# First pass of the mixer over five row tiles, two background pieces in the fourth product, attention's first left sides in the stage of v

## The chip, the cores and the metric

The kernel runs on one core of a Trainium2 chip. The metric is the device time of one execution in microseconds (us), from start to end; where several runs are given, their median. The engines are called PE (TensorE, matrix products), PEld (its weight loads), DVE (VectorE), ACT (ScalarE), POOL (GpSimd) and SP (SyncE, which mostly issues transfers). Each engine works through its own instructions in order, and semaphores hold an instruction until what it needs is done.

## What is computed

Two layers, each with a token mixer and a dense MLP. Every part is modulated by a vector c through adaLN (shift, scale, gate). Layer 0 mixes tokens by spatial gating, layer 1 by windowed attention with three dilations. Everything is float32.

```python
def ada_mod(c, w, b):
    m = jax.nn.silu(c) @ w + b
    shift, scale, gate = jnp.split(m, 3, axis=-1)
    return shift[:, None, :], scale[:, None, :], 1.0 + gate[:, None, :]

def mixer_a(h, w_in, b_in, vn_g, vn_b, w_s, b_s, w_out):
    uv = jax.nn.gelu(h @ w_in + b_in)
    u, v = jnp.split(uv, 2, axis=-1)
    v = layer_norm(v, vn_g, vn_b)
    ...
    w_causal = jnp.where(causal, w_s, 0.0)
    z = jnp.einsum('gts,bnsgc->bntgc', w_causal, v) + b_s.T[:, :, None]
    return (u * z) @ w_out

def reference(...):
    for i in range(DEPTH):
        shift, scale, gate = ada_mod(c, ada_w[i, 0], ada_b[i, 0])
        h = x * (1.0 + scale) + shift
        y = mixer_a(...) or mixer_b(h, b_w_qkv[j], b_w_out[j], slopes)
        x = layer_norm(ALPHA * x + gate * y, ln_g[i, 0], ln_b[i, 0])
        shift, scale, gate = ada_mod(c, ada_w[i, 1], ada_b[i, 1])
        h = x * (1.0 + scale) + shift
        y = jnp.square(jax.nn.relu(h @ mlp_w_up[i])) @ mlp_w_down[i]
        x = layer_norm(ALPHA * x + gate * y, ln_g[i, 1], ln_b[i, 1])
    return x
```

x is 1024 rows by 1024 columns (eight row tiles of 128, eight column tiles k of 128), ada_w is 1024 by 3072 for each part, the MLP is 4096 wide.

## The kernel before

The program runs `mixer_a`, `mlp(1)`, `attention` and `mlp(3)` one after the other. A float32 product is made as three products of fp32r parts: `split` (L103, L104) writes a high part by a cast on ACT and a low part by a subtraction on DVE, and high x high, high x low and low x high are summed in one PSUM bank of 128x512. So one row tile with one k and one half of the columns (`dh`) costs three products. A scheduler orders the instructions of an engine, except those marked by `keep_in_program_order` (`pin`, `pe`), which keep the order of the code among themselves.

**First pass of `mixer_a` (L545 to L622).** v = gelu(h w_in + b) is made for the first 512 columns (`dh` 0) in two passes over the rows: first tiles 0 to 3, then 4 to 7 (the list `others`). In the first pass the adaLN vector of the mixer, 2048 sums over 1024 weights, isn't there yet, so the pass goes by quarters q of the model dimension (two k each). For each quarter `load` issues on SP's queue the blocks of ada_w, the row tiles' columns and one block of w_in. `add` multiplies each ada_w block by silu(c) and adds it on DVE (L587), for k = 0 to 4 (`ON_DVE`); `total` sums over the partitions on PE: twelve narrow products (one column) of raw blocks for k = 5 to 7 (L596) and four of DVE's sums with ones (L597), which DVE then adds to the bias (`mod`, L599). `turn` transposes x on PE (L535), `scaled` applies the modulation on ACT (L541), `high` casts (L545), `low` subtracts (L548), and `v_sums` makes the products (L521). All of this is pinned. The next quarter's `add` stands between the other DVE work of this one. In the second pass nothing is pinned.

After it come the spatial weights: `ws` is loaded into the work tiles with tag "h", transposed on PE (L662, `psws`), copied, and masked on POOL, ahead of the products for `dh` 1.

**Background list.** The adaLN vectors of later parts are made in pieces (`ada_steps`, L112): a group is eight steps (a load of 128x512 on SP, L123, and one DVE operation, L126 or L129), a bias row, a `reduce` (split) and a `total` on PE (`psa`, L152 to L165). `tick(n)` runs the next n pieces, `drain` all that are left. In `mlp(1)` the list has ten groups, 110 pieces. Its up stage makes seven products p for each of 16 chunks (Strassen's scheme, L915), with the left sides of five products made ahead (`AHEAD`); after each product of chunks 2 to 15 (98) it runs one piece (L992), and drains the rest (L993) before the down stage (`psd`, L1073). In these parts of j of 2 and more the steps' DVE operations are pinned.

**Attention.** `values_stage` makes v (L1267 on PE), evicted by ACT's copies (L1275) or DVE's additions (L1283) and written out by POOL's transfers (L1287). Then the PSUM banks are opened anew (set "B") and `project` makes q and k by the same seven products (`psqk`, L1426). Its `load` and first three `make_left` (`AHEAD` is 3; `left`, by L103 and L104) come after that opening. In DVE's order `far` (L1448), a copy of a mask that POOL makes (`near`, L1444), stands ahead of the low parts of these left sides.

## Time and profile before

| | us |
|---|---|
| runs of before | 2630.4, 2636.0, 2635.61 (median 2635.61) |
| profiled execution: its time | 2630.7 |
| its span, first to last instruction | 2629.0 |
| mixer's first quarter: mod(0) on DVE | 20.24 |
| the last quarter: mod(3) | 58.80 |
| second pass: first product | 73.89 |
| attention: first psqk product | 1222.08 |

The page of the profile gives busy times by engine, the groups of instructions by line and the chain of work that ended last. Beside it the trace was asked for PE's waits, for windows (busy time of each engine between two times) and for timelines (single rows: start, length, engine, line, operation, output and inputs, shape, count, and in brackets the idle time before with what ended it).

### The profile page before, as it was taken

To read this page: it belongs to the slowest core of one execution; us is meant where nothing else is said; L and a number is where in the kernel's file an instruction comes from. 1 tells how busy PE (TensorE), PEld (TensorE's weight loads), DVE (VectorE), ACT (ScalarE), POOL (GpSimd) and SP (SyncE) were. 2 spreads that over 40 slices of the span, in tenths; PEclk is the share of its full clock that TensorE was granted. 3 is DMA by queue.
4 is the path that set the end of the run, shared out by engine and by line. 5 is a ranking of instruction groups with operands and counts; after the bars stand their busy time and mean duration, and the time that the engine had idled before them with its cause. 6 is when DMAs were issued, how large, how long until landed. Compare 5 with 4: busy or idle time off the path is not lost.

```text
span 2629.0 us, 36861 instructions
## 1 busy us (share of the span) xinstructions
PE 2582.9 (98%) x13322; PEld 2079.7 (79%) x13322; DVE 1897.3 (72%) x3510; ACT 1265.9 (48%) x2436; POOL 122.0 (5%) x181
## 2 busy tenths in 40 slices
PE   7999999999999999999999999999999999999998
PEld 6778878888788888887777777777777888878887
DVE  4677798787788778444677677777669856577987
ACT  2343275555433445322655556555517655543332
POOL 0001100000000000011011011010100000000000
PEclk8999999999999999999999999999999999999999
DMA  7454427666965644542344445454853654594562
GB/s 246 119 177 127 134 102 249 205 220 220 309 233 176 228 141 151 160 160 96 98 115 134 121 119 158 135 142 135 316 175 110 222 186 148 173 328 155 184 207 81
DMA packets 328779, 453.37 MB, mean 172 GB/s; under 512 B 51420, under 2 KB 179844, under 8 KB 328596
## 3 DMA queue, kind: packets, MB, share of 16 engines
q1 hardware_dynamic: 316692, 409.07, 48.8%
q0 software_dynamic: 11904, 41.95, 4.5%
q8 instruction: 104, 1.70, 0.3%
q14 instruction: 79, 0.65, 0.1%
HBM read 342.33 MB, written 108.61 MB: 172 GB/s over the span
## 4 chain that ended last, share of the span: by engine, by line
PE 82%; DVE 7%; issue 6%; DMA 3%; ACT 1%; POOL 1%; SPq 0%; DVEq 0%; POOLq 0%; ACTq 0%
PE psd L1073 20%; PE psqk L1426 18%; PE psua L915 11%; PE psuc L915 6%; PE psv L1267 4%; PE psv L521 3%; PE psd_wout L329 3%; PE psd_wo L329 3%; PE psub L915 3%; PE psu L329 3%; PE sc L1579 2%; PE pv L1619 2%; DMA adaw<-in_ada_w_dram 2%; PE pT L1590 1%; DVE right L104 1%
## 5 line engine op out<-in xcount | busy, mean ns | idle before, releaser
L1426 PE MATMUL psqk<-right,left 128*128 128x512 f32 x2016 | 523.1, 404 | 3.3 <-DVE left L104 2.2
L1426 PEld LDWEIGHTS psqk<-right,left 128*128 128x128 f32 x2016 | 363.1, 189 | 96.0 <-issue 14.9
L915 PE MATMUL psua<-right,left 128*128 128x512 f32 x1536 | 364.6, 391 | 3.2 <-ACT right L103 1.8
L1073 PE MATMUL psd<-rhi,lhi 128*128 128x512 f32 x896 | 350.8, 392 | 2.3 <-ACT part L946 2.1
L1073 PE MATMUL psd<-rlo,lhi 128*128 128x512 f32 x896 | 350.3, 391 | 0.7 <-DVE rlo L104 0.6
L1073 PE MATMUL psd<-rhi,llo 128*128 128x512 f32 x896 | 350.1, 391 | 0.0
L915 PEld LDWEIGHTS psua<-right,left 128*128 128x128 f32 x1536 | 287.1, 188 | 65.2 <-DVE right L104 2.6
L104 DVE TENSOR_TENSOR left<-ws,left 128x512 fp32r<-128x512 f32 x224 | 153.6, 687 | 141.4 <-ACT left L103 139.8
L1267 PE MATMUL psv<-vwhi,right 128*128 128x512 f32 x672 | 209.8, 393 | 0.0
L1493 ACT ACTIVATE p<-p,stat 128x256 f32<-128x256 f32 (+2 forms) x384 | 161.8, 423 | 90.7 <-DVE stat L1491 89.0
L1073 PEld LDWEIGHTS psd<-rhi,lhi 128*128 128x128 f32 x896 | 168.9, 189 | 38.7 <-ACT part L946 3.0
L1073 PEld LDWEIGHTS psd<-rlo,lhi 128*128 128x128 f32 x896 | 169.0, 189 | 36.6 <-DVE rlo L104 1.5
L1073 PEld LDWEIGHTS psd<-rhi,llo 128*128 128x128 f32 x896 | 168.9, 189 | 34.8
L915 PE MATMUL psuc<-right,left 128*128 128x512 f32 x768 | 189.5, 393 | 0.5 <-ACT right L103 0.4
L103 ACT CAST left<-ws 128x512 fp32r<-128x512 f32 x224 | 137.9, 620 | 102.5 <-DVE ws L836 73.7
L915 PEld LDWEIGHTS psuc<-right,left 128*128 128x128 f32 x768 | 144.5, 189 | 31.4 <-DVE right L104 0.9
L129 DVE SCALAR_TENSOR_TENSOR adaacc<-adaw,silu_c,adaacc 128x512 f32<-128x512 f32 x140 | 107.3, 766 | 63.3 <-DMA adaw<-in_ada_w_dram 62.3
L1267 PEld LDWEIGHTS psv<-vwhi,right 128*128 128x128 f32 x672 | 126.0, 188 | 28.0 <-ACT vwhi L103 0.2
L1491 DVE CUSTOM_DVE_ANT_0 p<-sc,bias 128x256 f32<-128x256 f32 (+2 forms) x384 | 103.5, 325 | 55.4 <-PE sc L1579 55.3
L104 DVE TENSOR_TENSOR llo<-lraw,lhi 128x1024 fp32r<-128x1024 f32 x112 | 136.2, 1216 | 1.5 <-ACT lhi L103 1.5
L1267 PE MATMUL psv<-vwlo,right 128*128 128x512 f32 x336 | 131.9, 394 | 0.2 <-DVE vwlo L104 0.2
L103 ACT CAST lhi<-lraw 128x1024 fp32r<-128x1024 f32 x112 | 117.3, 1048 | 7.6 <-PE psua L915 4.3
(266 smaller groups left out, 4354.1 us busy)
## 6 DMA issues: line engine op xcount, KB each, us to landing
lraw<-forms SPq DMA_DIRECT2D x112, 512.0 KB, 4.0
adaw<-in_ada_w_dram SPq DMA_DIRECT2D x192, 256.0 KB, 3.2
up<-in_mlp_w_up_dram SPq DMA_DIRECT2D x64, 512.0 KB, 3.9
forms<-s SPq DMA_DIRECT2D x128, 256.0 KB, 2.3
rraw<-in_mlp_w_down_dram SPq DMA_DIRECT2D x64, 512.0 KB, 5.9
forms<-part SPq DMA_DIRECT2D x96, 256.0 KB, 2.5
vraw<-in_b_w_qkv_dram SPq DMA_DIRECT2D x42, 512.0 KB, 4.0
spill<-acc SPq DMA_DIRECT2D x24, 512.0 KB, 2.6
```

Of the source, the lines that this page charges most:

```text
L103: first = A.copy(hi, src) if hi_engine is A else hi_engine.tensor_copy(hi, src)
L104: return first, lo_engine.tensor_tensor(lo, src, hi, op=ALU.subtract)
L129: ins = V.scalar_tensor_tensor(acc[:], raw[:], silu_c[:, k : k + 1], acc[:], ALU.mult, ALU.add)
L329: T.matmul(dst, s[a], m[b], start=(n == 0), stop=(n == last))
L521: pin(T.matmul(sums[half, dh, i][:], hT[half][a][:, k, i * P : (i + 1) * P], w[b][:, k % 2, :], start=k == 0 and a + b == 0, stop=k == KD ...
L915: T.matmul(acc, w[:, a, k, :], right[p][:, b, k, :], start=p in (1, 2, 5) and k + a + b == 0, stop=k == 3 and a == 1, skip_group_check=True)
L1073: T.matmul(sums[kind, m][:], l[a][:, k, m * P : (m + 1) * P], r[b][:, k, :], start=p in (1, 5, 2, 3) and kp + k + a + b == 0, stop=kp == K ...
L1267: T.matmul(sums[own, m][:], right[p][:, b, 2 * kp + k, m * P : (m + 1) * P], w[a][:, k, :], start=new and k + a + b == 0, stop=kp + k == 2 ...
L1426: ins = T.matmul(sums[kind][:], w[:, a, k, :], right[p][:, b, k, :], start=p in (1, 2, 5) and k + a + b == 0, stop=k == 3 and a == 1, skip ...
L1491: V.tensor_tensor_reduce(out=pr, in0=src, in1=bias, scale=-0.125, scalar=3e38, op0=ALU.add, op1=ALU.min, accum_out=nm)
L1493: A.activation(pr, pr, AF.Exp, bias=nm, scale=-1.0, accum_out=l)
L1579: pe(T.matmul(scb[e][:, sl], my["q"][rows, t * P : (t + 1) * P], my["k"][rows, k0 : k0 + w], start=True, stop=True))
```

## The change

1. The mixer's first pass takes five row tiles (`FIRST`), the second three. The row tiles' columns are loaded on POOL's queue (`nc.gpsimd`), ahead of the ada_w blocks in the code; a block of ada_w is now one k with both parts (128x2x256, 256 KB), and the loads of w_in are pinned too. `add` covers all eight k, with one operation 512 wide for both parts. `total` is left with four narrow products, written into the third transposing bank (`extra`), which also holds the fifth tile's transposes; the transposes now stand ahead of the sums. The last tile of `others` no longer takes a tile of the pool `ada0`.
2. The spatial weights' loads and transposes are spread over the k of `dh` 1 (half 1).
3. In the up stage of `mlp` the fourth product of a chunk runs two pieces of the background list.
4. `project` is defined ahead of `values_stage`; its first loads (into work tiles with tag "res") and the first two left sides are issued within the last steps of that stage, the third after the banks are opened.

Parts of the diff (the definitions that only move are left out):

```diff
+            def v_sums(dh, k, rows_, pin=free):
                 w = w_units[dh, k // 2]
-                for i in range(4):
...
-                ON_DVE = 5
+                FIRST = range(5)
...
-
-                    for kk in range(3):
-                        for part in (1, 0):
-                            block(kk, part)
-                    w = slice(q * QUARTER, (q + 1) * QUARTER)
-                    for i in range(4):
-                        pin(nc.sync.dma_start(tiles[i][:, w], x_in[i * P : (i + 1) * P, w]))
-                    w_raw[q] = v_raw(0, q)
-                    for part in (1, 0):
-                        block(3, part)
+                    cols_ = slice(q * QUARTER, (q + 1) * QUARTER)
+                    parts = ada_w[0, 0].rearrange("k (s n) -> k s n", n=D)[:, 0:2, cols_]
+
+                    def block(k):
+                        t = raws[q, k] = ada0.tile([P, 2, QUARTER], F32, name=f"adaw_0_{q}_{k}", tag="adaw", bufs=16)
+                        pin(nc.sync.dma_start(t[:], parts[k * P : (k + 1) * P]))
+
+                    for i in FIRST:
+                        pin(nc.gpsimd.dma_start(tiles[i][:, cols_], x_in[i * P : (i + 1) * P, cols_]))
+                    for k in range(KD - 2):
+                        block(k)
+                    w_raw[q] = v_raw(0, q, pin)
+                    for k in range(KD - 2, KD):
+                        block(k)
 
...
                 def add(q, ks):
                     for k in ks:
-                        for part in (1, 0):
...
-
-                def total(q):
-                    pst = bank("tr", f"psa_0_{q}")
-                    for part in range(2):
+                        if k == 0:
+                            accs[q] = ada0.tile([P, 2, QUARTER], F32, name=f"adaacc_0_{q}", tag="adaacc")
+                            pin(V.tensor_scalar(accs[q][:], raws[q, 0][:], silu_c[:, 0:1], None, ALU.mult))
+                        else:
+                            acc = accs[q][:]
+                            pin(V.scalar_tensor_tensor(acc, raws[q, k][:], silu_c[:, k : k + 1], acc, ALU.mult, ALU.add))
+
+                def total(q, pst):
+                    for s in range(2):
                         for n in range(2):
-                            c = slice(2 * part + n, 2 * part + n + 1)
+                            c = slice(2 * P + 2 * s + n, 2 * P + 2 * s + n + 1)
                             w = slice(n * P, (n + 1) * P)
-                            for k in range(ON_DVE, KD):
-                                pin(T.matmul(pst[:, c], raws[q, part, k // 2][:, k % 2, w], silu_c[:, k : k + 1], start=k == ON_DVE, stop=False))
-                            pin(T.matmul(pst[:, c], accs[q, part][:, w], ones_f[:, 0:1], start=False, stop=True))
+                            pin(T.matmul(pst[:, c], accs[q][:, s, w], ones_f[:, 0:1], start=True, stop=True))
...
-                add(0, range(ON_DVE))
                 load(1)
+                add(0, range(KD - 2))
+                every = slice(0, HALF)
                 for q in range(4):
-                    total(q)
-                    psts = [turn(0, k, tiles, pin) for k in (2 * q, 2 * q + 1)]
-                    h = scaled(0, 2 * q, psts[0], pin)
-                    high(0, 2 * q, h, pin)
+                    k0, k1 = 2 * q, 2 * q + 1
+                    psts = [bank("tr", f"pst_0_{k}") for k in (k0, k1)]
+                    for k in (k0, k1):
+                        turn(psts[k % 2], 0, k, tiles[:4], pin)
+                    extra = bank("tr", f"pst_0_x{q}")
+                    for k in (k0, k1):
+                        turn(extra, (k % 2) * P, k, tiles[4:], pin)
+                    add(q, range(KD - 2, KD))
+                    v_split(0, q, w_raw[q], pin)
+                    total(q, extra)
+                    h = [h_tile(f"h_0_{k}") for k in (k0, k1)]
+                    scaled(h[0][:], psts[0][:], k0, pin)
+                    high(0, k0, every, h[0][:], pin)
                     if q:
-                        v_sums(0, 0, 2 * q - 1, pin)
+                        v_sums(0, k0 - 1, FIRST, pin)
                     if q < 3:
-                        add(q + 1, range(2))
-                    low(0, 2 * q, h, pin)
-                    v_split(0, q, w_raw[q], pin)
-                    h = scaled(0, 2 * q + 1, psts[1], pin)
-                    high(0, 2 * q + 1, h, pin)
+                        add(q + 1, range(1))
+                    low(0, k0, every, h[0][:], pin)
+                    scaled(h[1][:], psts[1][:], k1, pin)
+                    high(0, k1, every, h[1][:], pin)
                     if q < 3:
-                        add(q + 1, range(2, 3))
-                    low(0, 2 * q + 1, h, pin)
-                    v_sums(0, 0, 2 * q, pin)
+                        add(q + 1, range(1, 2))
+                    low(0, k1, every, h[1][:], pin)
+                    hx = h_tile(f"h_0_x{q}")
+                    for k in (k0, k1):
+                        w = slice((k % 2) * P, (k % 2 + 1) * P)
+                        scaled(hx[:, w], extra[:, w], k, pin)
+                    both = hx[:, 0 : 2 * P].rearrange("p (k c) -> p k c", c=P)
+                    high(1, slice(k0, k1 + 1), slice(0, P), both, pin)
+                    low(1, slice(k0, k1 + 1), slice(0, P), both, pin)
+                    v_sums(0, k0, FIRST, pin)
                     if q < 2:
                         load(q + 2)
                     if q < 3:
-                        add(q + 1, range(3, ON_DVE))
-                v_sums(0, 0, KD - 1, pin)
+                        add(q + 1, range(2, KD - 2))
+                v_sums(0, KD - 1, FIRST, pin)
...
-                others = [work.tile([P, D], F32, name=f"x0_{4 + i}", tag="res", bufs=3) for i in range(3)]
-                others.append(ada0.tile([P, D], F32, name="x0_7", tag="x0"))
+                others = [work.tile([P, D], F32, name=f"x0_{5 + i}", tag="res", bufs=3) for i in range(3)]
                 for i, t in enumerate(others):
-                    nc.sync.dma_start(t[:], x_in[(4 + i) * P : (5 + i) * P, :])
-                v_end(0, 0)
+                    nc.sync.dma_start(t[:], x_in[(5 + i) * P : (6 + i) * P, :])
+                v_end(0, FIRST)
+                rest = slice(P, HALF)
                 for k in range(KD):
-                    h = scaled(1, k, turn(1, k, others))
-                    high(1, k, h)
-                    low(1, k, h)
-                    v_sums(1, 0, k)
-                v_end(1, 0)
+                    pst = bank("tr", f"pst_1_{k}")
+                    turn(pst, P, k, others)
+                    h = h_tile(f"h_1_{k}")
+                    scaled(h[:, rest], pst[:, rest], k)
+                    high(1, k, rest, h[:, rest])
+                    low(1, k, rest, h[:, rest])
+                    v_sums(0, k, range(5, NT))
+                v_end(0, range(5, NT))
...
+                raw_s = {}
+
+                def spatial_load(q):
+                    ws = raw_s[q] = work.tile([P, 4, P], F32, name=f"ws_{q}", tag="h")
                     nc.sync.dma_start(ws[:], a_w_s[0, 4 * q : 4 * q + 4].rearrange("g t s -> t g s"))
+
+                def spatial(q):
+                    ws = raw_s.pop(q)
...
+                        if half and 3 <= k < 7:
+                            spatial(k - 3)
+                        if half and 1 <= k < 5:
+                            spatial_load(k - 1)
+                        v_sums(1, k, range(4 * half, 4 * half + 4))
...
-                        tick()
+                        tick(2 if p == 4 else 1)
...
+            def two(name):
+                t = work.tile([P, 2, 4, P], F32, name=name, tag="res", bufs=3)
+                return [t[:, 0], t[:, 1]]
...
+                lefts = [(n, p) for n in range(len(order)) for p in (1, 2, 6, 5, 7, 4, 3)]
+                yield
+                for s in lefts[: AHEAD - 1]:
+                    make_left(*s)
+                yield
+                make_left(*lefts[AHEAD - 1])
...
+                        if n in (len(steps) - LOADS, len(steps) - SPLITS):
+                            next(stream)
...
-                for s in lefts[:AHEAD]:
-                    make_left(*s)
```

**Place 1: PE, the first pass, about the sums of quarter 1.** The first rows are the second half of the sum. Names: psv are the sums of v (row tile in the name), psa the modulation's sums, adaacc DVE's sums, pst the banks of the transposes. Before:

```order
L597 MATMUL psa_1_283<-ones_f,adaacc_1_0_226 128x1
L596 MATMUL psa_1_283<-silu_c,adaw_1_1_2_178 128x1
L596 MATMUL psa_1_283<-silu_c,adaw_1_1_3_188 128x1 x2
L597 MATMUL psa_1_283<-ones_f,adaacc_1_1_224 128x1
L596 MATMUL psa_1_283<-silu_c,adaw_1_1_2_178 128x1
L596 MATMUL psa_1_283<-silu_c,adaw_1_1_3_188 128x1 x2
L597 MATMUL psa_1_283<-ones_f,adaacc_1_1_224 128x1
L535 MATMUL pst_0_2_302<-ident,x_0_132 128x128
```

Now, where pst_x is the fifth row tile's bank:

```order
L522 MATMUL psv_4_247<-winv_0_hi,hT_1_1_124 128x512
L535 MATMUL pst_2_278<-ident,x_0_132 128x128
L535 MATMUL pst_2_278<-ident,x_1_133 128x128
L535 MATMUL pst_2_278<-ident,x_2_134 128x128
L535 MATMUL pst_2_278<-ident,x_3_135 128x128
L535 MATMUL pst_3_279<-ident,x_0_132 128x128
L535 MATMUL pst_3_279<-ident,x_1_133 128x128
L535 MATMUL pst_3_279<-ident,x_2_134 128x128
L535 MATMUL pst_3_279<-ident,x_3_135 128x128
L535 MATMUL pst_x_288<-ident,x_4_136 128x128 x2
L591 MATMUL pst_x_288<-ones_f,adaacc_1_219 128x1 x4
L522 MATMUL psv_0_231<-winv_0_hi,hT_0_0_121 128x512
```

The twelve products with adaw are gone, the four with adaacc are left, and the transposes, ten instead of eight, stand ahead of them.

**Place 2: PE, between the up and the down stage of the first MLP.** psa_0_1 is the last sum of the background list (hi and lo parts of adaacc), psu the up stage's products, psd the down stage's. Before, inside the down stage:

```order
L1073 MATMUL psd_1_0_5971<-rhi_1_3_6041,llo_1_3_6038 128x512
L1073 MATMUL psd_1_1_5975<-rhi_1_3_6041,lhi_1_3_6037 128x512
L1073 MATMUL psd_1_1_5975<-rlo_1_3_6042,lhi_1_3_6037 128x512
L160 MATMUL psa_0_1_5890<-ones_r,adahi_0_1_5886 128x2
L1073 MATMUL psd_1_1_5975<-rhi_1_3_6041,llo_1_3_6038 128x512
L1073 MATMUL psd_1_2_5979<-rhi_1_3_6041,lhi_1_3_6037 128x512
L1073 MATMUL psd_1_2_5979<-rlo_1_3_6042,lhi_1_3_6037 128x512
L1073 MATMUL psd_1_2_5979<-rhi_1_3_6041,llo_1_3_6038 128x512
```

Now, inside the up stage:

```order
L937 MATMUL psua_15_5688<-right_7_3168,left_15_7_5685 128x512 x12
L937 MATMUL psuc_15_5733<-right_3_2971,left_15_3_5707 128x512 x12
L160 MATMUL psa_0_1_5834<-ones_r,adahi_0_1_5806 128x2
L937 MATMUL psua_15_5688<-right_4_3169,left_15_4_5730 128x512
L161 MATMUL psa_0_1_5834<-ones_r,adalo_0_1_5807 128x2
```

The sum moved from between products of the down stage to between the last two products of the up stage.

**Place 3: DVE, the end of v's stage in attention.** vwlo is the low part of the last weights of v, v_0 the evictions of v, left the low parts of q's and k's left sides, ws sums of weights, far the copy that waits for POOL. Before:

```order
L104 TENSOR_TENSOR vwlo_4_1_9930<-vraw_4_1_0_9891,vwhi_4_1_9929 128x1024
L1283 TENSOR_TENSOR v_0_0_9782<-psv_0_0_9653,v_0_0_9782 128x512
L1283 TENSOR_TENSOR v_0_1_9784<-psv_0_1_9657,v_0_1_9784 128x512
L1283 TENSOR_TENSOR v_0_2_9786<-psv_0_2_9661,v_0_2_9786 128x512
L1283 TENSOR_TENSOR v_0_3_9788<-psv_0_3_9665,v_0_3_9788 128x512
L1448 COPY far<-near 64x64 x2
L104 TENSOR_TENSOR left_2_1_10024<-wq_0_2_10016,left_2_1_10024 128x512
L104 TENSOR_TENSOR left_2_2_10027<-wq_0_2_10018,left_2_2_10027 128x512
L1370 TENSOR_TENSOR ws_2_6_10030<-wk_0_2_10020,wk_0_2_10022 128x512
L1198 TENSOR_TENSOR ws_2_6_10031<-ws_2_6_10030,wq_0_2_10016 128x512
```

Now:

```order
L1440 TENSOR_TENSOR v_0_0_9745<-psv_0_0_9616,v_0_0_9745 128x512
L1440 TENSOR_TENSOR v_0_1_9747<-psv_0_1_9620,v_0_1_9747 128x512
L1440 TENSOR_TENSOR v_0_2_9749<-psv_0_2_9624,v_0_2_9749 128x512
L1440 TENSOR_TENSOR v_0_3_9751<-psv_0_3_9628,v_0_3_9751 128x512
L104 TENSOR_TENSOR left_2_2_9929<-wq_2_9896,left_2_2_9929 128x512
L1292 TENSOR_TENSOR ws_2_6_9991<-wk_2_9899 128x512
L1220 TENSOR_TENSOR ws_2_6_9991<-ws_2_6_9991,wq_2_9896 128x512
L104 TENSOR_TENSOR left_2_6_9994<-ws_2_6_9991,left_2_6_9994 128x512
L104 TENSOR_TENSOR left_2_5_10001<-ws_2_6_9991,left_2_5_10001 128x512
L1220 TENSOR_TENSOR ws_2_7_10033<-wk_2_9899,ws_2_6_9991 128x512
L1220 TENSOR_TENSOR ws_2_6_9991<-wq_2_9896,ws_2_6_9991 128x512
L1485 COPY far<-near 64x64 x2
```

The low parts of the left sides 1, 2, 6 and 5 now stand ahead of far; left_2_1's stands in the row ahead of the first one shown, ahead of the last evictions of v.

More of the change, by code (lines that the diff above doesn't have):

```diff
@@ L522, in v_sums, with v_end @@
                                      start=k == 0 and a + b == 0, stop=k == KD - 1 and a == 1))
[L524 removed]
+            def v_end(dh, rows_):
                 w = slice(dh * HALF, (dh + 1) * HALF)
[L526 to L528 removed]
+                for r in rows_:
+                    z = vz[:, r, w]
+                    V.tensor_tensor(z, sums.pop((dh, r))[:], v_bias[:, w], op=ALU.add)
@@ L538, in scaled @@
-            def scaled(half, k, pst, pin=free):
-                h = work.tile([P, HALF], F32, name=f"h_0_{half}_{k}", tag="h")
+                    pin(T.transpose(pst[:, c0 + n * P : c0 + (n + 1) * P], t[:, k * P : (k + 1) * P], ident[:]))
+            def scaled(dst, src, k, pin=free):
                 m = mods[k // 2]
-                pin(A.activation(h[:], pst[:], AF.Identity, bias=m[:, k % 2 : k % 2 + 1], scale=m[:, 2 + k % 2 : 3 + k % 2]))
-                return h
-            def high(half, k, h, pin=free):
-                pin(A.copy(hT[half][0][:, k, :], h[:]))
@@ L547, in low, with high @@
-            def low(half, k, h, pin=free):
-                pin(V.tensor_tensor(hT[half][1][:, k, :], h[:], hT[half][0][:, k, :], op=ALU.subtract))
-            with tc.tile_pool(name="ada0", bufs=2, reuse_waits="tile") as ada0:
-                ON_DVE = 5
+                pin(A.activation(dst, src, AF.Identity, bias=m[:, k % 2 : k % 2 + 1], scale=m[:, 2 + k % 2 : 3 + k % 2]))
+            def high(half, ks, cols_, h, pin=free):
+                pin(A.copy(hT[half][0][:, ks, cols_], h))
+            def low(half, ks, cols_, h, pin=free):
+                pin(V.tensor_tensor(hT[half][1][:, ks, cols_], h, hT[half][0][:, ks, cols_], op=ALU.subtract))
@@ L553, in pin, with h_tile @@
+            def h_tile(name):
+                return work.tile([P, HALF], F32, name=name, tag="h")
+            with tc.tile_pool(name="ada0", bufs=3, reuse_waits="tile") as ada0:
+                FIRST = range(5)
                 def pin(ins):
@@ L1206, in values_stage @@
+            stream = project()
             def values_stage():
@@ L1328, in by_pos @@
-            def by_pos(t, g):
-                if g == 0:
-                    return t
-                if g == 1:
-                    return t.rearrange("p (i r) -> p r i", r=4)
-                return t.rearrange("p (i b a) -> p a b i", b=2, a=8)
-            order = [(hp, g) for hp in range(N_PAIRS) for g in PATTERNS]
-            got = [dict() for _ in order]
-            pinned = []
-            def quarter(name):
-                return qp.tile([P, 4, P], F32, name=name, tag="wq", bufs=4)
```

241 lines of the change are left out of this document (117 added, 124 removed).

## The prediction

> **What bounds the kernel.** I read the busy times first, then what TensorE (PE) waited for, then windows over the stretches that the change touches.
>
> ```profile
> PE 2582.9 (98%) x13322; PEld 2079.7 (79%) x13322; DVE 1897.3 (72%) x3510; ACT 1265.9 (48%) x2436; POOL 122.0 (5%) x181
> ```
>
> PE is busy for 98% of the span, so a faster vector or scalar engine brings nothing by itself. Time can come only from three places: PE work that is dropped, PE idle time, and PE work done at a low granted clock. Which waits exist, the view of PE's waits says (what waited, for what: us in all, times, the longest):
>
> ```profile
> PE psa L596 <- DMA adaw<-in_ada_w_dram: 8.2, 2, 4.8
> PE psqk L1426 <- DVE left L104: 2.2, 1, 2.2
> PE psqk L1426 <- ACT left L103: 1.2, 1, 1.2
> PE psws L662 <- DMA ws<-in_a_w_s_dram: 0.9, 1, 0.9
> ```
>
> What a dense product costs, and what it costs at the low clock, two rows of the chain of work that ended last show (start, length, engine, what, count):
>
> ```profile
> 24.88 5.06 PE psv L521 x11
> ...
> 74.04 13.79 PE psv L521 x60
> ```
>
> At full clock a 128x512 product takes 13.79/60 = 0.230 us; in the first stretch it took 5.06/11 = 0.46, exactly twice.
>
> **Mixer, first pass: the sums for the modulation.** Windows on PE's psa work alone, one for each quarter (sum, PE, PEld, DVE, mean granted clock, DMA share, GB/s):
>
> ```profile
> 13.60:20.10 6.50, 6.46 (x30) 6.46 (x30) 0.00 (x0) 1.00 1.01 321
> 29.70:33.40 3.70, 3.67 (x32) 3.66 (x31) 0.00 (x0) 1.00 1.01 330
> 41.30:46.00 4.70, 4.62 (x32) 4.66 (x32) 0.00 (x0) 0.75 0.99 342
> 54.40:58.70 4.30, 4.21 (x32) 4.23 (x32) 0.00 (x0) 0.83 0.01 4
> ```
>
> The four stretches hold PE for 6.5 + 3.7 + 4.7 + 4.3 = 19.2 us (the first mostly waits for adaw). The change leaves 8 of 32 records: 3.67 x 8/32 = 0.9 us each at the rate of the second, some 1.7 at half clock. In exchange DVE adds all eight k instead of five. So the period of a quarter passes from PE to DVE, and I add up DVE's and ScalarE's (ACT's) chain. Groups by form (count | busy, mean ns | idle before):
>
> ```profile
> L129 DVE SCALAR_TENSOR_TENSOR adaacc<-adaw,silu_c,adaacc 128x512 f32<-128x512 f32 x70 | 52.3, 747 | 23.7 <-DMA adaw<-in_ada_w_dram 23.4
> L126 DVE TENSOR_SCALAR adaacc<-adaw,silu_c 128x512 f32<-128x512 f32 x10 | 4.8, 478 | 0.0
> L548 DVE TENSOR_TENSOR hT<-h,hT 128x512 fp32r<-128x512 f32 x10 | 6.8, 687 | 5.2 <-ACT hT L545 5.2
> L104 DVE TENSOR_TENSOR winv_lo<-winv_raw,winv_hi 128x1024 fp32r<-128x1024 f32 x4 | 4.9, 1225 | 1.0 <-ACT winv_hi L103 0.8 <-DMA x<-in_x_dram 0.3
> L541 ACT ACTIVATE h<-pst,mod 128x512 f32<-128x512 f32 x16 | 12.1, 774 | 46.2 <-PE pst L535 45.3 <-DVE hT L548 0.9
> L545 ACT CAST hT<-h 128x512 fp32r<-128x512 f32 x16 | 9.6, 619 | 0.3
> ```
>
> From one modulation (mod) to the next: scale 0.77 and cast 0.62 on ACT, low part 0.69 on DVE; the add of k=1, 0.75; the second low part until 3.7; the fifth row's narrow scale, cast and low part (no such form before; between nothing and three full operations of 2.1, I take 0.8, by width) until 4.5; six adds of 0.75 until 9.0; the split of w_in 1.23, beside which PE's short sum lies; then mod. That is 10.3, and I take 10.5. PE has 30 products x 0.23 = 6.9, ten transposes of 0.12 (1.47/12, row below) and the sum of 0.9 in that time, 9.0 at full clock: it fits, closely. The row tile that is new in this pass so costs PE nothing here.
>
> Next, when the first quarter can begin. The start's windows (PE, PEld, DVE, ACT, POOL, then clock, DMA share, GB/s) and mod's rows:
>
> ```profile
> 0.00:10.00 10.00, 0.71 (x3) 0.48 (x3) 4.81 (x18) 1.49 (x2) 0.70 (x6) 1.00 0.67 203
> 10.00:20.00 10.00, 6.65 (x32) 6.56 (x32) 0.27 (x1) 0.00 (x0) 0.00 (x0) 1.00 1.03 338
> 20.00:30.00 10.00, 7.93 (x24) 6.00 (x24) 6.37 (x14) 3.64 (x5) 0.00 (x0) 1.00 1.02 328
> ...
> 20.24 0.16 DVE L599 TENSOR_TENSOR mod<-psa,bias 128x4 f32<-128x4 f32 x1 [9.97 <-PE psa L597]
> ...
> 58.80 0.16 DVE L599 TENSOR_TENSOR mod<-psa,bias 128x4 f32<-128x4 f32 x1 [5.06 <-PE psa L597]
> ```
>
> From 10 to 30 us the 16 DMA engines are full, at 338 GB/s. All 2.62 MB of x (five rows, four quarters) now stands at the head of GpSimd's (POOL's) queue, beside 2.62 MB of quarter 0 on SP's. If both share the engines evenly, 5.24 MB must have moved: 2.03 MB by 10 us, the other 3.21 MB at 0.338 MB/us by 19.5 us. One add, the sum and mod: 21.3, a little later than the 20.24 of before. Bounds are 16 (x takes nothing from SP) and 25 (x goes ahead of it). The Trainium skill ("DMA: Bandwidth & Descriptors", Issuing engines are not separate DMA queues) says that DMAs of every issuing engine run on the same 16 engines and interleave, and that a second issuer saves only issue time. By that rule the move itself buys nothing and mod stands at 21.3; without it at 16, five us better. That the share was full with SP alone speaks for the rule; how POOL's packets mix in, no row of before shows.
>
> How long POOL takes to issue, a later place shows:
>
> ```profile
> 1054.20 2.58 POOL L1287 DMA_DIRECT2D v_dram<-v  x4 [8.28 <-DVE v L1283]
> ```
>
> That is 0.65 us each, 13 us for the 20; they wait for nothing, and nothing else that POOL does is needed in this stage. Then mod(3) = 21.3 + 11.5 (a cold first quarter, as the row of x11 shows) + 10.5 + 10.5 = 53.8 against 58.80. Behind it stand 45 products, 10.4, and about 0.9 of low clock: the pass ends at 65. Before:
>
> ```profile
> 70.44 1.47 PE L535 MATMUL pst<-ident,x 128*128 128x128 f32 x12
> ...
> 73.89 0.50 PE L521 MATMUL psv<-winv_hi,hT 128*128 128x512 f32 x1
> ```
>
> The second pass's products then begin at 65 + 3.1 = 68.1 (3.45 before, less one row's share of the first transposes), not at 73.89: 5.8 gained. It has three rows, not four: 24 products less, 5.5, and 0.4 of transposes. Together 11.7; I take **11.5** (7 to 15). The move of the spatial loads takes away the wait of psws: **0.9**.
>
> **MLP: two pieces in the fourth product.** The background list of 110 pieces has 98 places in the up stage; 12 are drained after it, and the last sum of the list then stands among the down products. With two pieces in 14 places there are 112. The windows at that place, and the wait:
>
> ```profile
> 684.00:688.00 4.00, 2.81 (x13) 2.00 (x11) 1.80 (x3) 2.12 (x2) 0.00 (x0) 1.00 0.98 309
> 688.00:692.00 4.00, 2.11 (x13) 1.93 (x14) 3.01 (x6) 1.08 (x2) 0.00 (x0) 1.00 1.01 388
> 692.00:696.00 4.00, 4.00 (x12) 3.09 (x12) 4.00 (x6) 2.68 (x3) 0.00 (x0) 0.57 1.05 393
> ...
> 689.89 0.27 PE L160 MATMUL psa<-ones_r,adahi 128*128 128x2 f32 x1 [3.08 <-ACT adahi L103]
> ```
>
> In these 12 us PE did 38 records, 8 of them the narrow sum: 30 products, 6.9 us at full rate. 5.1 are lost, first by waiting, then at a clock of 0.57. The sum itself, 0.9, only moves: **4.2** (2 to 5). It could wait in the up stage as well, for an adaw that lands late; that would be some 1 us.
>
> **Attention: the first left sides.** At the opening PE waits twice:
>
> ```profile
> 1218.82 2.69 ACT L1275 COPY v<-psv 128x512 f32<-128x512 f32 x4 [19.19 <-PE psv L1267]
> 1222.08 0.73 PE L1426 MATMUL psqk<-right,left 128*128 128x512 f32 x2 [1.19 <-ACT left L103]
> ...
> 1223.80 0.39 DVE L1448 COPY far<-near 64x64 f32<-64x64 f32 x2 [13.42 <-POOL near L1444]
> ...
> 1224.96 11.39 PE L1426 MATMUL psqk<-right,left 128*128 128x512 f32 x42 [2.15 <-DVE left L104]
> ```
>
> The casts stand behind ACT's copies of v, the low parts behind DVE's copy far, which waits for POOL. With both made ahead of that, 44 products run from 1220.89 (1222.08 less 1.19) and end after 44 x 0.23 = 10.1 at 1231.0; they ended at 1224.96 + 11.39 = 1236.35. That is **5.2** (3 to 5.4): 3.3 of waiting, the rest low clock. The DVE work ahead of far is cover for the third left side; if it lay late, the 2.15 would come back.
>
> **Sum.** 11.5 + 0.9 + 4.2 + 5.2 = 21.8. The profiled execution took 2630.7 (its span 2629.0): 2608.9. The runs of before lie at 2630.4, 2635.61 and 2636.0, so their median is 4.9 above the profiled one, and the sum would be 2613.8 from there. I forecast **2611**, between the two, nearer the profile.
>
> **Rivals.**
> Low clock in each quarter: ten transposes and a sum stand between the products in every quarter, and after such stretches (41 to 46 us) the clock was 0.75. If each of the three later quarters loses what the 11 products at half rate lost (5.06/2 = 2.5), it is 7.6 less the 0.9 that I allowed, 6.7: 2618. The Trainium skill ("TensorE: Matmul & The Clock Gate", Part 1: The HAM clock gate) says that the clock is reconsidered in windows of about 3.4 us, and halves after an idle one. The trace agrees, with 0.46 beside 0.230 us for a product; by that rule a quarter in which PE idles little, 1.5 of 10.5 us, would mostly keep its clock, which is why this is not the forecast. Chance 0.2.
> x ahead of adaw: mod(0) at 25, or SP's blocks starved in a later quarter, 4 to 7 us: 2616 to 2618. For it: the share is full for 30 us. Against: POOL's issues come one in 0.65 us, so that x is spread over 13 us. Chance 0.12.
> Parts that don't do what they say: the third left side still late (2.2 and its low clock), or the last sum waits among the up products: 2 to 4 us, 2614. Chance 0.1.
> POOL's queue takes nothing from SP's: mod(0) at 16, 2606. Chance 0.1.
> Slower: the additions of the background list are pinned on DVE in program order, so one that waits for its adaw holds what is queued behind it, the low parts of the next left sides, and PE waits for these.
>
> ```profile
> adaw<-in_ada_w_dram SPq DMA_DIRECT2D x192, 256.0 KB, 3.2
> ```
>
> With two pieces in 14 places, each could wait the 3.2 us of a landing: 44.8. Less the other 17.6 that is 27 slower: 2658. It decides once the waits exceed the cover of five products made ahead, 5 x 12 x 0.23 = 13.8 us. One landing is far below that. Chance 0.03.
>
> **How the numbers follow.** The forecast's own case (2606 to 2614) has 0.45. Range 2602 to 2621: it takes in the good rival and the two at 2616 to 2618. About 0.2% (5.3 us) is what a measurement of this kernel can tell from no change; slower 0.03, within it 0.03 (two of the larger rivals together with weak gains elsewhere), faster 0.94.
>
> **What would show it.** mod(0) near 21 and mod(3) near 54 in the rows of DVE; psa's windows of 1 to 2 us each; the second pass's products from 68; DMA share full until 20 in the first windows; no idle time at the opening of attention and 44 products in 10 us; no psa among the down products. Wrong it would be if mod's period is over 12, if the clock is below 0.8 in every quarter, or if DVE waits long for adaw in the MLP's up stage.

## The result and the profile after

| | before | after |
|---|---|---|
| median of the runs, us | 2635.05 (4 runs) | 2613.59 (4 runs, 2611.85 to 2616.89) |
| ratio, 95% interval | | 0.9924 (0.9906 to 0.9941) |
| profiled execution: time, span | 2630.7, 2629.0 | 2611.85, 2610.1 |

The change makes the kernel 0.8% faster in this comparison, and 0.6% in a second one (after_again below). The page of the profile after, the line of busy times by engine:

```profile
PE 2561.9 (98%) x13226; PEld 2058.5 (79%) x13226; DVE 1902.3 (73%) x3506; ACT 1267.7 (49%) x2448; POOL 132.8 (5%) x201
```

PE lost 96 records (the 12 narrow products of four quarters, recorded twice each) and 21 us of busy time; DVE's busy time is 5 us longer, and POOL has its 20 issues more. PE's waits after, those that answer to the ones of before:

```profile
PE pst_x L591 <- DVE adaacc L584: 10.3, 2, 9.0
...
PE psa L161 <- DVE adalo L104: 1.8, 2, 1.5
...
PE psa L160 <- ACT adahi L103: 1.2, 2, 0.8
```

The waits for adaw, for the left sides and for ws are gone. The first row is the start of the first quarter (9.0) and a wait of 1.2 in the third. The two rows of psa are four waits in the up stage of the first MLP (0.23 + 0.43 + 1.54 + 0.78 = 3.0 us), where the kernel before has none; of them more below.

**The first pass.** The modulation's rows on DVE (start, length, engine, line, operation, what, count, idle time before), and two windows of the start:

```profile
21.74 0.16 DVE L593 TENSOR_TENSOR mod<-pst_x,bias 128x4 f32<-128x4 f32 x1 [0.82 <-PE pst_x L591]
...
32.04 0.16 DVE L593 TENSOR_TENSOR mod<-pst_x,bias 128x4 f32<-128x4 f32 x1
...
42.35 0.16 DVE L593 TENSOR_TENSOR mod<-pst_x,bias 128x4 f32<-128x4 f32 x1
...
52.76 0.16 DVE L593 TENSOR_TENSOR mod<-pst_x,bias 128x4 f32<-128x4 f32 x1
```

```profile
0.00:10.00 10.00, 2.56 (x9) 1.60 (x10) 2.72 (x11) 1.49 (x2) 6.92 (x18) 1.00 0.73 218
10.00:20.00 10.00, 0.96 (x5) 0.56 (x3) 4.48 (x7) 1.04 (x1) 4.72 (x9) 1.00 1.07 359
```

mod(0) stands at 21.74, the period is 10.3, mod(3) at 52.76: forecast were 21.3, 10.5 and 53.8. The three middle intervals have the same length to 0.1 us and the rows 2 to 4 show no idle time before them: DVE works without a break toward mod, as the sum of its chain said. In the first 20 us PE does almost nothing (3.5 of 20 us), and from 10 to 20 us the DMA share is 1.07.

**Between the stages of the first MLP, and inside the up stage.** Windows (sum, PE, PEld, DVE, ACT, POOL, clock, DMA share, GB/s), first the stretch behind the up stage, then two inside it:

```profile
682.00:686.00 4.00, 4.00 (x20) 3.30 (x19) 0.82 (x1) 2.00 (x2) 0.00 (x0) 1.00 1.04 393
```

```profile
598.00:602.00 4.00, 2.02 (x12) 1.56 (x12) 3.98 (x9) 1.70 (x4) 0.00 (x0) 1.00 0.71 240
602.00:606.00 4.00, 4.00 (x13) 3.10 (x12) 2.54 (x5) 2.15 (x4) 0.00 (x0) 0.61 0.98 313
```

The loss between the stages is gone, as forecast. A new one stands inside the up stage: PE idles for half of one window and runs at a clock of 0.61 in the next. The rows around it, on PE and on DVE:

```profile
598.53 0.27 PE L160 MATMUL psa<-ones_r,adahi 128*128 128x2 f32 x1 [0.43 <-ACT adahi L103]
600.68 0.27 PE L161 MATMUL psa<-ones_r,adalo 128*128 128x2 f32 x1 [1.54 <-DVE adalo L104]
```

```profile
597.07 0.75 DVE L129 SCALAR_TENSOR_TENSOR adaacc<-adaw,silu_c,adaacc 128x512 f32<-128x512 f32 x1 [1.91 <-DMA adaw<-in_ada_w_dram]
...
599.94 0.69 DVE L104 TENSOR_TENSOR adalo<-adaacc,adahi 128x512 fp32r<-128x512 f32 x1
```

The last addition of a background sum waited 1.91 us for its adaw; its low part came 2.9 us later, behind other work of DVE; and the sum's products, which the order has between products of the up stage, held PE.

**Attention.** PE's row and one of ACT's:

```profile
1207.15 13.07 PE L1351 MATMUL psqk<-right,left 128*128 128x512 f32 x56
```

```profile
1195.88 0.62 ACT L103 CAST left<-wq 128x512 fp32r<-128x512 f32 x1 [4.82 <-PE psv L1424]
```

56 products of psqk run without a break, 0.233 us each, and the left side was cast 11 us ahead of them.

### The profile page after: what moved, and what is told of

It is laid out like the page before. It is cut to its first block, busy times and chain, and to the rows that moved or that the text cites. A ratio compares the mean times of both kernels' runs of the same rounds, so it can differ in the third digit from the quotient of the medians.

```text
span 2610.1 us, 36711 instructions
## 1 busy us (share of the span) xinstructions
PE 2561.9 (98%) x13226; PEld 2058.5 (79%) x13226; DVE 1902.3 (73%) x3506; ACT 1267.7 (49%) x2448; POOL 132.8 (5%) x201
## 4 chain that ended last, share of the span: by engine, by line
PE 85%; DVE 7%; DMA 4%; ACT 2%; issue 1%; SPq 0%; DVEq 0%; ACTq 0%
PE psd L1095 23%; PE psqk L1351 17%; PE psua L937 10%; PE psv L1424 9%; PE psuc L937 5%; PE psu L329 3%; DMA adaw<-in_ada_w_dram 3%; PE psd_wout L329 3%; PE psd_wo L329 3%; PE psub L937 2%; PE sc L1616 2%; PE pv L1656 2%; PE psv L522 1%; PE pT L1627 1%; DVE right L104 1%; DVE left L104 1%
```

## The experiments

The total times scatter by some 5 us from run to run, so beside the ratios I use the starts of the same PE instructions in the profiles. In this table u is the first product of psu (end of the mixer's v stage), MLP the time from the first psua product to the 101st psd product (the background list's last sum lies in it), attention that from the 1001st product of psv in the program (the 617th of attention) to the 45th of psqk. The three times of a row are those of one profile.

| run | what it is | u, us | MLP, us | attention, us | ratio to before (95%) |
|---|---|---|---|---|---|
| before | | 147.9 | 349.7 | 105.8 | 1 |
| after | the change | 135.4 | 350.5 | 100.4 | 0.9924 (0.9906 to 0.9941) |
| after_again | the change | 133.5 | 352.7 | 100.4 | 0.9941 (0.9928 to 0.9954) |
| e1_one_piece | part 3 undone | 135.1 | 354.4 | 100.4 | 0.9940 (0.9924 to 0.9955) |
| e2_spaced | split a piece earlier | 135.3 | 349.6 | 100.4 | 0.9938 (0.9924 to 0.9951) |
| e3_x_on_sp | x on SP | 134.8 | 351.7 | 100.4 | 0.9951 (0.9937 to 0.9965) |
| e4_four_rows | four row tiles | 136.5 | 353.0 | 100.4 | 0.9969 (0.9958 to 0.9981) |
| e6_all_dve | before, sums on DVE | 138.6 | 351.2 | 106.0 | 0.9985 (0.9974 to 0.9996) |
| e11_late_sums | sums two pieces later | 133.8 | 347.8 | 100.4 | 0.9917 (0.9904 to 0.9930) |
| e9_three_bufs | three adaw buffers | 131.1 | 345.3 | 100.4 | 0.9898 (0.9885 to 0.9910) |
| e10_three_bufs_one | the same, part 3 undone | 132.0 | 351.0 | 100.4 | 0.9922 (0.9906 to 0.9939) |
| e13_three_bufs_x | e9, later x on SP | 128.6 | 347.2 | 100.4 | 0.9897 (0.9880 to 0.9914) |
| e15_bufs_x_sp | e9, all x on SP | 129.7 | 346.9 | 100.4 | 0.9899 (0.9882 to 0.9916) |
| e14_four_rows_bufs | e9, four row tiles | 133.0 | 345.2 | 100.4 | 0.9914 (0.9897 to 0.9931) |

The start of the first quarter scatters too, which u contains: in the seven profiles whose first pass is the same code (after, after_again, e1, e2, e11, e9, e10) mod(0) stands at 19.6 to 21.7 us. Where it matters I also count u from the run's own mod(0).

**Part 3 undone.**

```diff
-                        tick(2 if p == 4 else 1)
+                        tick()
```

> The change with one background piece after every product again (part 3 undone). By the prediction's term, part 3 is worth 4.2 us, so this is 4.2 slower than the changed kernel, about 2618. By the ledger of the two traces, part 3 gave its gain between the stages back inside the up stage (a wait of 1.5 us on adalo at 600.7 us and a half-clock window from 602.9 us, then a wait of 0.8 at 656.6): the two cancel, this runs within 1 us of the changed kernel, 2613, with a half-clock window shortly after the up stage and none near 600 us.

The medians agree within the scatter, 2612.89 here and 2613.97 for the change run once more (the kernel before had 2630.07 and 2630.05 beside them). In the trace the up stage is clean, and the loss stands behind it again. PE's row with the wait, and the windows around it:

```profile
677.62 0.37 PE L160 MATMUL psa<-ones_r,adahi 128*128 128x2 f32 x1 [3.08 <-ACT adahi L103]
```

```profile
676.00:680.00 4.00, 2.38 (x8) 1.99 (x8) 2.71 (x4) 1.66 (x2) 0.00 (x0) 0.58 1.02 380
680.00:684.00 4.00, 4.00 (x13) 3.42 (x14) 2.76 (x5) 2.09 (x2) 0.00 (x0) 0.50 1.06 395
684.00:688.00 4.00, 4.00 (x13) 3.11 (x13) 2.01 (x2) 0.76 (x1) 0.00 (x0) 0.64 1.05 392
```

The wait is the 3.08 us of before, to the digit, but the low clock behind it lasts longer: the three windows add up to 10.2 us at half rate, and before it was 3.4 (4 us at 0.57). That is why the MLP takes 354.4 us here (one short stretch of low clock near 363 us, 1.6, is in it too), against 349.7 in the kernel before with the same order. Against this run, part 3 brought 1.7 to 3.9 us (1.7 to 2.3 without the stretches of 1.6 near 363 us here and near 360 us in after_again); against the one profile of before, nothing.

**The split a piece earlier.**

```diff
-            todo.append([lambda k=k, step=step: step(k) for k in range(KD)] + [bias_row, reduce, total])
+            todo.append(steps_[:-1] + [lambda s=steps_[-1], r=bias_row: (s(), r()), reduce, lambda: None, total])
```

(The second line holds for the parts of j of 2 and more; the others keep the first.)

> The change, with one empty piece between the split of a background sum (reduce) and its psa products on PE; the bias row's piece is joined to the eighth addition, so there are still 110 pieces. If psa comes too close behind its split, PE gains a product of 2.7 us as cover: the waits at 600.7 and 656.6 and the half-clock window go, 5 to 6 us less, about 2608. If instead DVE is simply too far behind in that stage, the waits turn up at other products and the time stays within 2 us of 2613.

Neither: the waits did not go, nor did they move.

```profile
598.60 0.27 PE L160 MATMUL psa<-ones_r,adahi 128*128 128x2 f32 x1 [0.29 <-ACT adahi L103]
600.75 0.27 PE L161 MATMUL psa<-ones_r,adalo 128*128 128x2 f32 x1 [1.54 <-DVE adalo L104]
```

An earlier split can't start before the last addition, and that one waits for its adaw. So it is not the distance of split and sum in the list that decides; the distance of the last addition and the sum, three pieces, is the same in both. The theory of the expectation fell. (No low-clock window followed here, which alone is worth some 1.5 us.)

**x on SP's queue.**

```diff
-                    for i in FIRST:
-                        pin(nc.gpsimd.dma_start(tiles[i][:, cols_], x_in[i * P : (i + 1) * P, cols_]))
                     for k in range(KD - 2):
                         block(k)
+                    for i in FIRST:
+                        pin(nc.sync.dma_start(tiles[i][:, cols_], x_in[i * P : (i + 1) * P, cols_]))
```

> The change with the five x loads of a quarter on SP's queue again, behind the six first adaw blocks of that quarter. If queue and issuing engine matter little because the 16 engines are full (share 1.07 from 10 to 20 us), mod(0) stays at 20 to 22 us and the time within 2 us of 2613. If POOL's queue takes the x bytes of later quarters in front of adaw, mod(0) comes some 3 to 5 us earlier here and the time is 2609 to 2611. If SP's issue time (20 issues of 0.5 us or more) is what counts, mod comes later by 3 or more in each quarter and the time is over 2618.

The four rows of mod together (count: least, median and longest ns; first and last start):

```profile
L593 DVE TENSOR_TENSOR mod<-pst_x,bias x4: 160/163/164, 21.7 to 52.7; 128x4 f32<-128x4 f32 x4
```

The modulation comes at the same times. But the run tells less than it was meant to: with SP's pinned loads changed, the scheduler had put two whole row tiles of the second pass (1 MB) ahead of x on SP. e15 below repeats it with that order held.

**Four row tiles in the first pass.**

```diff
-                FIRST = range(5)
+                FIRST = range(4)
...
-                    v_sums(0, k, range(5, NT))
+                    v_sums(0, k, range(4, NT))
```

(The fifth tile's transposes and narrow operations are left out, and a fourth tile is loaded for the second pass.)

> The change with four row tiles in the first pass and four in the second; the rest as changed. If DVE's chain sets a quarter (10.3 us, of which the fifth row's narrow operations are 0.9), mod(3) comes some 2.6 us earlier and the second pass takes 5.9 us longer: 3.3 slower than the changed kernel, about 2617. If PE's products set it, each quarter is 1.4 us shorter and nearly all of the 5.9 is won back: 2613 to 2615. If five rows bring their full 5.9: 2619.

The rows of mod together, and a row of PE in the u stage:

```profile
L593 DVE TENSOR_TENSOR mod<-pst_x,bias x4: 161/162/163, 21.4 to 49.8; 128x4 f32<-128x4 f32 x4
```

```profile
161.24 0.27 PE L160 MATMUL psa<-ones_r,adahi 128*128 128x2 f32 x1 [1.93 <-ACT adahi L103]
```

mod(3) comes 2.9 us earlier, near the 2.6 of the first case: DVE's chain sets a quarter. At u the loss is 1.0 us against the first profile of the change (2.9 against the second); counted from each run's own mod(0) it is 1.4 and 1.6. The rest of the 7 us by which the medians differ comes later: a late background split in the u stage (the second row) and low clock behind it, and a longer MLP.

**The change again, and the sums two pieces later.**

```diff
-            later(ada_steps(2, MODS + GATE) + ada_steps(3, MODS))
+            groups = ada_steps(2, MODS + GATE) + ada_steps(3, MODS)
+            for g in range(len(groups) - 1):
+                groups[g + 1].insert(2, groups[g].pop())
+            groups[-1].insert(len(groups[-1]) - 1, lambda: None)
+            later(groups)
```

> The changed kernel once more, beside the next three on one chip, so that they can be compared with it directly: 0.992 of the kernel before.

> The change with each background sum's psa products run two pieces later than now (after the second addition of the next group), the last one a piece later. e2 left psa in its place on PE, since it only moved the split. If psa waits because the last addition, held by a late adaw, leaves its split too little time, two more products (5.5 us) cover it: the waits at 600.7 and 656.6 us go, the half-clock window near 603 too, the MLP keeps 4 to 6 us more than the changed kernel, in all 0.2% less. If PE waits for DVE in that stage anyway, nothing changes.

The change again: 2613.97, and 2608.38 with the later sums (before 2630.05). The MLP takes 347.8 us instead of 350.5 and 352.7. The sum that waited now reads:

```profile
601.01 0.17 PE L160 MATMUL psa<-ones_r,adahi 128*128 128x2 f32 x1
```

No idle time stands before it, nor before any other sum of that stage. So the new waits can be covered by moving the sum, which is what e2 failed to do. A wait of 1.15 us for an eviction by DVE (at 650 us) and a stretch of low clock at 657 us are left.

**Three buffers for adaw.**

```diff
-                raw = ada_p.tile([P, HALF], F32, name=f"adaw_{nm}_{k}", tag="adaw", bufs=2)
+                raw = ada_p.tile([P, HALF], F32, name=f"adaw_{nm}_{k}", tag="adaw", bufs=3)
```

(The bias row, which takes a tile with the same tag, has 3 too.)

> The change with three buffers for the background list's adaw blocks, not two, so that a load can be issued one piece earlier. If the late adaw is the cause of the waits of psa, DVE's wait of 1.9 us ahead of the addition at 597 us goes and with it the 2.0 us of psa's wait and the half-clock window: 4 to 5 us less in the MLP. If the place of psa alone decides, the waits stay.

The cause itself: groups by form of DVE in the up stage (340 to 665 us), first of before (count | busy, mean ns | idle before):

```profile
L129 DVE SCALAR_TENSOR_TENSOR adaacc<-adaw,silu_c,adaacc 128x512 f32<-128x512 f32 x63 | 47.0, 746 | 19.0 <-DMA adaw<-in_ada_w_dram 18.7
```

of after:

```profile
L129 DVE SCALAR_TENSOR_TENSOR adaacc<-adaw,silu_c,adaacc 128x512 f32<-128x512 f32 x70 | 52.3, 747 | 25.4 <-DMA adaw<-in_ada_w_dram 25.2
```

and of this run:

```profile
L129 DVE SCALAR_TENSOR_TENSOR adaacc<-adaw,silu_c,adaacc 128x512 f32<-128x512 f32 x70 | 52.1, 744 | 8.8 <-DMA adaw<-in_ada_w_dram 8.8
```

DVE's waits for adaw rose from 18.7 to 25.2 us with the denser list and fall to 8.8 with a third buffer. By themselves they hold PE little: they are 28.4 us in e11, where no sum waits. They cost where a sum stands close behind the addition that waits. With the third buffer PE has no wait in the two windows that were shown of the change:

```profile
598.00:602.00 4.00, 4.00 (x20) 3.30 (x19) 0.31 (x1) 1.87 (x4) 0.00 (x0) 1.00 0.47 157
602.00:606.00 4.00, 4.00 (x19) 3.32 (x18) 3.18 (x6) 1.81 (x4) 0.00 (x0) 1.00 0.40 133
```

The MLP takes 345.3 us, 5.2 and 7.4 less than in the two profiles of the change. u comes 2.4 to 4.3 us earlier; from each run's own mod(0) it is 1.9 and 2.1 (111.6 us, beside 113.5 and 113.7), and the list does run in that stretch of the mixer too; the rest is the scatter of the start. No low clock is left before the end of the program. The median is 2603.06, 11 us below the change beside it: the fastest version of this study but for two that equal it.

**The kernel before with all sums on DVE.**

```diff
-                ON_DVE = 5
+                ON_DVE = 8
```

(The product with ones, now the first of its column, gets `start=True`.)

> The kernel before with one number changed: all eight k of the modulation are added on DVE (ON_DVE 8 for 5), the twelve narrow products with adaw are gone; four row tiles, x on SP, nothing else. e4 says that this is most of the mixer's gain (mod(3) at 49.8 with four rows): mod(3) at 49 to 52 us instead of 58.8, and 8 to 11 us less at the first psu product. By the prediction's split (5.0 from the earlier mod(3), the rest from fewer products behind it) only 5 to 6 would be won.

The rows of mod together, and PE's row at the opening of attention:

```profile
L599 DVE TENSOR_TENSOR mod<-psa,bias x4: 160/163/163, 16.9 to 50.2; 128x4 f32<-128x4 f32 x4
```

```profile
1217.61 12.74 PE L1426 MATMUL psqk<-right,left 128*128 128x512 f32 x47 [2.15 <-DVE left L104]
```

One number brings mod(3) to 50.2 and u 9.3 us forward, of the 12.5 to 14.4 that the change wins there. Of it 3.4 lie in the first modulation (16.9, not 20.24), 5.2 in the three periods behind it. The waits of attention's opening are those of before, so that stretch takes 106.0 us: parts 1 and 4 show apart. By the end of the program, though, only 3.2 us are left in the profile and 2.4 in the medians: the MLP is 1.6 longer than in the profile of before, the rest of attention gives back 1.7 and its output product (psd_wo) 4.9, with low clock from 1880.9 and 1966.3 us, in code that is the same; the second MLP returns 2.4.

**Three buffers, part 3 undone.** The edits of e9 and e1 together.

> Three buffers for the background list's adaw blocks, and one piece after every product (part 3 undone). Beside the run with three buffers and part 3 (e9) it tells what part 3 is worth once the late adaw is out of the way. By the prediction's term 4.2 us are lost again between the stages: the MLP keeps 4 to 5 us less than e9's, the time is 4 us above e9's, near 2607. If most of the loss between the stages was the late adaw too, the two are equal within 1 us.

```profile
670.10 0.27 PE L160 MATMUL psa<-ones_r,adahi 128*128 128x2 f32 x1 [4.22 <-ACT adahi L103]
```

The wait between the stages is back, longer than before, with low clock behind it:

```profile
668.00:672.00 4.00, 1.90 (x9) 1.75 (x10) 0.69 (x1) 2.62 (x3) 0.00 (x0) 0.86 1.03 392
672.00:676.00 4.00, 4.00 (x11) 3.26 (x12) 3.21 (x5) 2.43 (x3) 0.00 (x0) 0.50 1.05 393
676.00:680.00 4.00, 4.00 (x15) 3.20 (x14) 2.88 (x3) 0.70 (x1) 0.00 (x0) 0.79 1.05 389
```

The MLP takes 351.0 us: 5.7 more than with part 3 (345.3). The medians are 2609.46 and, for e9 on another chip, 2603.06 (on the same chip as e10, e13 and e15 below, which have part 3, are at 2602.8). So in this pair part 3 is worth what was forecast and more, once the adaw of its pieces is in time; how much more hangs on how long the low clock lasts.

**Where x is loaded, and four rows once more,** all on three buffers. In e13 x of quarter 0 is on POOL and the rest on SP behind six adaw blocks; in e15 all of it is on SP there, with the second pass's loads held in the code's order; e14 is e4 with three buffers.

> Three buffers (e9), and of x only quarter 0 on POOL's queue; the later quarters' five loads stand on SP's queue behind six adaw blocks of their quarter. If the 2.0 MB of x for later quarters, which now stand in the engines with quarter 0's blocks, hold up mod(0), it comes at 16 to 18 us instead of 21.7 and the kernel is 3 to 5 us faster than e9, about 2599. If all that is issued by then shares the engines whatever its queue, blocks of quarter 1 take their place and mod(0) stays at 20 to 22.

> Three buffers (e9), and all of x on SP's queue behind six adaw blocks of its quarter, with the loads for the second pass held in the order of the code. e3 didn't separate the queue from the order, since two whole row tiles of the second pass had moved ahead of x on SP. If order and bytes decide, not the queue: like e13, mod(0) at 16 to 18 us and about 2599. If a second issuing queue is worth something, mod(0) is 2 us or more later than in e13.

> Three buffers (e9) and four row tiles in the first pass (as e4). In e4 the fifth row tile was worth 1.0 us at the first psu product and the rest of e4's loss was a wait of psa on a late split (161 us) with a half-clock window behind it. With three buffers that wait should go: 1 to 3 us slower than e9. By the prediction's term, nine tenths of 5.9 us slower.

The rows of mod together, in e9:

```profile
L593 DVE TENSOR_TENSOR mod<-pst_x,bias x4: 162/163/163, 19.6 to 50.5; 128x4 f32<-128x4 f32 x4
```

in e13 (x of quarter 0 on POOL):

```profile
L597 DVE TENSOR_TENSOR mod<-pst_x,bias x4: 162/163/163, 16.9 to 47.9; 128x4 f32<-128x4 f32 x4
```

in e15 (all on SP):

```profile
L593 DVE TENSOR_TENSOR mod<-pst_x,bias x4: 161/162/163, 18.0 to 49.1; 128x4 f32<-128x4 f32 x4
```

and in e14 (four rows):

```profile
L593 DVE TENSOR_TENSOR mod<-pst_x,bias x4: 162/163/164, 20.5 to 49.0; 128x4 f32<-128x4 f32 x4
```

With the later quarters' x behind adaw blocks on SP, the first modulation comes 1.6 to 2.7 us earlier than in e9, and u with it (1.5 and 2.5). e9's 19.6 is the earliest of the seven starts with x on POOL's queue, and e6, which has x (of four rows) behind blocks on SP too, starts at 16.9. So the 2.0 MB of x for later quarters did hold up the start when they were issued beside the first blocks; the engines are no less full without them (share 1.08 from 10 to 20 us in e13, 1.07 in e9). Their queue and their place changed together, so which of the two did it is not shown; for quarter 0's own x the two queues differ by 1.1 us (16.9 and 18.0), which is within the scatter. The whole time does not show the gain: 2602.76 and 2602.87 beside e9's 2603.06. In both profiles a stretch of low clock near 356 us, in the up stage, takes 1.6 us back, and another near 1998 us stands in the second MLP; e9's profile has neither. Four rows cost 1.9 us at u (1.0 from mod(0)), and 2606.29 for the whole, with intervals that overlap e9's.

## Why the time was right and two of its terms were not

The forecast was 2611 and the median 2613.59. The sum was 21.8, and the two profiled executions differ by 18.9 (2630.7 less 2611.85): 14.0 in the mixer, 5.4 at attention's opening, 0.9 lost in the MLP, 0.4 elsewhere. So one term failed and another gave more than was counted. That the medians differ by 21.5 (2635.05 less 2613.59), nearly the sum, is luck: in the repetition it is 16.1 (2630.05 less 2613.97).

**Start and period of the quarters: right.** mod(0), the period, mod(3) and the first product of the second pass came at 21.7, 10.3, 52.8 and 66.0 where 21.3, 10.5, 53.8 and 68.1 stood; the 1.0 for a cold first quarter did not come (32.04 less 21.74 is 10.3), though its first products start 0.43 us apart, nor did the 0.9 of low clock behind mod(3): DVE, not PE, sets the period. That mod(0) lies within 0.5 us of its sum is partly luck, since the same start gave 19.6 to 21.7. At the first psua product the mixer is 14.0 us ahead (348.1 less 334.1), against 11.5 and 0.9. One reading was loose: the slow products of the kernel before start 0.43 us apart too, not 0.46, and the clock column says 1.00 over that stretch (20 to 30 us), so there the products and not the column tell the clock.

**What the fifth row brings: wrongly apportioned.** The prediction counted 5.9 for the second pass's fourth row tile, with its transposes. That is so against the second pass of before, but it is not what the row brings: with four rows a quarter is 0.8 us shorter ((49.8 - 21.4)/3 = 9.5 beside 10.3), since the row's narrow operations lie in DVE's chain, and mod(3) came 2.9 (e4) and 1.5 (e14) earlier. The row is worth 1.0 to 2.9 us (e4) and 1.9 (e14) at u, or 1.0 to 1.6 counted from mod(0). The main part is the sums' move from PE to DVE, 9.3 us with a single number (e6). The statement that the row "costs PE nothing" holds; DVE pays for it.

**Part 3: the step that was mis-sized.** The prediction gave 4.2 and, for a wait in the up stage "for an adaw that lands late", some 1 us. Measured: the loss between the stages went as forecast, but the waits inside were 3.0 us, with a window of 13 records where 19 fit behind them, 6 x 0.23 = 1.4: 4.4 together, all that had been won. The MLP as a whole lost 0.9 (after) and 3.1 (after_again, 1.6 of it the low clock near 360 us) against before instead of winning 4.2. The rival "Parts that don't do what they say" had this wait, for the last sum among the up products, at 2 to 4 us and 2614, with a chance of 0.1; here the last sum waited 0.78 (656.6 us) and an earlier one 1.97 (598.5 to 600.7). The slower rival named the mechanism, pinned additions that wait for adaw and hold what is queued behind them; but it looked at the left sides, which five products cover, and not at the sum's own split, which one product covers. And one of the signs of being wrong came: DVE waited longer for adaw in that stage, 25.2 us for 18.7. e11, e9 and e10 settle it: with the sum moved, or with a third buffer, the waits go, and with the buffer part 3 brings 5.7.

**Attention: right.** 5.4 us (105.8 less 100.4), in every run with the part and not in e6, which is without it; 5.2 was forecast.

**Spatial loads:** the wait of 0.9 is gone from PE's list; it was not tried alone.

**Rivals.** Low clock in each quarter did not come: one stretch, at 43 us, in the profile of after, none there in after_again. x ahead of adaw (mod(0) at 25) and a POOL queue that takes nothing from SP's (16) both fell: mod(0) lay between, and came earlier once the later x was taken from POOL's queue (e13, e15). The rule of the Trainium skill ("DMA: Bandwidth & Descriptors", Issuing engines are not separate DMA queues) that all issuers share the 16 engines agrees with the DMA share from 10 to 20 us, full with POOL and SP issuing (1.07, 352 GB/s in e9) and as full with SP alone (1.04, 344 GB/s in e15). The equal medians, 2602.76, 2602.87 and 2603.06, don't test it.

## What to carry to other kernels

A background list that is made denser may need its loads made deeper with it: here two pieces in a row with two buffers raised DVE's waits for the loads from 18.7 to 25.2 us, and what was held first was the piece with the least cover, the sum, not the main work. Either remedy took the waits of the sum away, more cover (e11) or earlier loads (e9). To say what one part of a change is worth, ask what sets the period with and without it, not how much work it takes from a later stage. And a gain that is won by closing a short PE wait is a gain of the wait and of the low clock behind it; the second is not a fixed price.

## What the runs showed of the hardware beside that

The price of one wait of PE in low clock varies. The same 3.08 us before the last background sum was followed by 3.4 us of half clock in the kernel before (a window of 4 us at 0.57) and by 10.2 us in e1 (0.58, 0.50, 0.64). Short waits elsewhere, as the 2.0 us at 600 us, brought a stretch of half clock in the two profiles of the change and none in e2, with waits of about the same length (0.29 and 1.54). And at one place of the up stage, some 28 us behind its first product, low clock came in five of the fourteen profiles (after_again, e1, e4, e13, e15); each time it cost 1.6 us against e9, where it did not come. It is one reason why stretches with the same order differ by some us from profile to profile. An idle window, by which the prediction reckoned, is not needed for it: the longest of the waits at 600 us is 1.54 us. What decides over it was not tried.
